# LayerNorm of a convolution branch inside a projection stage: gates loaded a chunk ahead, the next mean ahead of this variance, affine part on ScalarE

## The chip, the cores and the metric

The kernel runs on one core of a Trainium2 chip. The metric is device time in microseconds (us) for one execution. Engines: TensorE (PE, matmuls and transposes), VectorE (DVE), ScalarE (ACT), GpSimd (POOL) and SyncE (SP), whose queue issues the DMAs of this stage. Each engine takes its instructions in a fixed order that is set when the program is built.

## The reference, cut to what matters

One layer of a streaming encoder over a sequence of 2048 positions with 1024 channels. An input projection gives, among others, the input and the gate of a convolution branch (512 channels), queries, keys and values of an attention branch, its gate, and two merge gates. The branch that the change touches:

```
u = depthwise_causal_conv(glu(u), width 31) + b_dw
mu  = mean over 512 channels of u
xc  = u - mu
var = mean over channels of xc*xc
n   = xc * rsqrt(var + EPS) * ln_g + ln_b        # layer_norm
za  = silu(n) * silu(gate_A)                     # silu(n) = n * sigmoid(n)
y_A = za @ w_conv_out
```

Then stick-breaking attention over eight heads, the merge y = sigmoid(m_A) * y_A + sigmoid(m_B) * y_B, and the output projection with a residual.

## The kernel before, in words

All matmuls of the projections are in a split form: every float32 operand is a high part and a remainder, and a product is three matmuls (`mm3`, L135). Channels lie on the 128 partitions, the sequence is cut into four chunks of 512 columns (`CH`), and a projection block is one 128-channel slice of the output for one chunk: 24 matmuls of 512 columns into a PSUM tile `pd`, of which there are five.

The stages: inputs and modulation; projections with the convolution taps on VectorE (here the convolution's gates `ga` are computed, and stored to DRAM already as silu); then the stage of this case (L720 to L868); then attention, with the remaining merge gates as filler; then the output projections.

In the stage of this case three things are written by hand in turn. `v_group(5)` (L831) computes six half-blocks of values and stores them through tiles `st` (two of them, 128 x 1024); `gate_b(2)` and `gate_b(3)` compute the attention gate (L841), `merge_gate` three merge gate slices (L852). Each of these blocks ends in an evacuation by ScalarE (`vsg`, L847 or L858) and a store, and then calls `next(ln)`, which advances the generator `ln_all` (L775) by one step. So the LayerNorm of the four chunks is woven between blocks. Its steps for a chunk:

- mean: `ln_load` fetches four 128 x 512 tiles `cv` (one for each 128 channels, two sets); `presum` (L744) adds the four into `t1`, two on GpSimd (L747), two and the total on VectorE (L748, L749); `mean_in` splits the sum into `hl` (L770 on ScalarE, L771 on VectorE); two matmuls with a constant matrix of 1/512 give the mean on all partitions, `mub` (L783).
- centering: VectorE subtracts (L788), ScalarE squares (L790, into tiles `sq0` to `sq3`), `presum` adds the squares.
- three steps (blocks) later the variance: four narrow matmuls into `pst` (L798), EPS added (L800), an inverse square root by integer start and three Newton steps on 128 x 4 values (`rsqrt`, L81 to L93), four scaled identity matrices `dg` (L755).
- one block later (two for the second chunk) `spread` (L759) multiplies them with ones into `psb`: the inverse deviation on all partitions.
- normalizing, for each of the four tiles: VectorE multiplies by `psb` (L809); GpSimd applies gain and bias (L810); the convolution's gate is loaded into `gt`, a single tile (L814); ScalarE takes the Sigmoid into `lsg`, which has the buffer of that tile's square (L816); GpSimd multiplies (L817); VectorE multiplies by the gate (L819); SyncE stores `za` (L823).
- the mean of the next chunk (L825), and one more block.

The builder orders each engine's instructions from this program; within the stage TensorE is kept in the order that is written, and the other engines' work is fitted in by priority and by when operands come free. A tile that is allocated again waits for all uses of its former content.

Of the kernel before, what the change touches and what calls it, by code (L numbers as in the profile page):

```python
# [8 lines left out]
F32 = mybir.dt.float32  # L9
# [3 lines left out]
AF = mybir.ActivationFunctionType  # L13
ALU = mybir.AluOpType
# [4 lines left out]
P = 128  # L19
SEQ = 2048  # L20
D = 1024
KC = D // P
CH = 512
NCH = SEQ // CH
# [26 lines left out]
def trunk_kernel(  # L51
# [20 lines left out]
    nc = tc.nc  # L72
# [85 lines left out]
    ga_d = [[dram(f"ga{j}_{g}", [P, CH], F32) for g in range(NCH)] for j in range(JC)]  # L158
# [27 lines left out]
    with ExitStack() as s1:  # L186
# [221 lines left out]
        with tc.tile_pool(name="hx", reuse_waits="tile", bufs=1) as hx:  # L408
# [53 lines left out]
            for i in range(2):  # L462
# [5 lines left out]
                for k in (2 * i, 2 * i + 1):  # L468
# [4 lines left out]
                    else:  # L473
                        dve.scalar_tensor_tensor(out=sq, in0=xs[k], scalar=1.0, in1=xs[k],
                                                 op0=ALU.mult, op1=ALU.mult,
                                                 accum_out=ss[:, k:k + 1])
                if i == 0:
# [4 lines left out]
                                     op0=ALU.add, op1=ALU.mult)  # L482
# [14 lines left out]
            for kc in range(KC):  # L497
                col = slice(kc, kc + 1)
                if kc == 0:
                    cast(wq[0], w2_q0[0])  # L500
                act.activation(out=b_s[:, col], in_=mod[:, col], func=AF.Identity,
                               bias=ba[:, col])
# [217 lines left out]
        with ExitStack() as sl:  # L720
# [21 lines left out]
                return cv  # L742

            def presum(tiles):  # L744
                t1 = lp.tile([P, CH], F32, tag="t1", name="t1")
                t2 = lp.tile([P, CH], F32, tag="t2", name="t2")
                nc.gpsimd.tensor_tensor(out=t1, in0=tiles[0], in1=tiles[1], op=ALU.add)  # L747
                nc.vector.tensor_tensor(out=t2, in0=tiles[2], in1=tiles[3], op=ALU.add)  # L748
                nc.vector.tensor_tensor(out=t1, in0=t1, in1=t2, op=ALU.add)  # L749
                return t1  # L750
# [16 lines left out]
            def mean_in(cv):  # L767
                t1 = presum(cv)
                hl = lp.tile([P, 2, CH], F32R, tag="hl", name="hl")
                nc.scalar.copy(out=hl[:, 0, :], in_=t1)  # L770
                nc.vector.tensor_tensor(out=hl[:, 1, :], in0=t1, in1=f(hl[:, 0, :]),  # L771
                                        op=ALU.subtract)
                return hl

            def ln_all():  # L775
                cv = ln_load(ORDER[0])
                yield
                hl = mean_in(cv)
                yield
                for n_, g in enumerate(ORDER):  # L780
                    mub = pm.tile([P, CH], F32, tag="psb", name="mub")
                    for i in range(2):
                        mm(mub, onesr, hl[:, i, :], start=(i == 0), stop=(i == 1))  # L783
                    if n_ + 1 < NCH:
                        nxt = ln_load(ORDER[n_ + 1])
                    sqs = []
                    for j in range(JC):
                        nc.vector.tensor_tensor(out=cv[j], in0=cv[j], in1=mub, op=ALU.subtract)  # L788
                        sq = lp.tile([P, CH], F32, tag=f"sq{j}", name=f"sq{j}")
                        nc.scalar.activation(out=sq, in_=cv[j], func=AF.Square)  # L790
                        sqs.append(sq)
                    t1 = presum(sqs)
                    yield
                    yield
                    yield
                    vs = pm.tile([P, 4], F32, tag="pst", name="pst")
                    for i in range(4):
                        mm(vs[:, i:i + 1], t1[:, i * P:(i + 1) * P], invc, start=True, stop=True)  # L798
                    va = sm.tile([P, 4], F32, tag="va", name="va")
                    nc.vector.tensor_scalar(out=va, in0=vs, scalar1=EPS, scalar2=None,  # L800
                                            op0=ALU.add)
                    dg = diag(rsqrt(sm, va, 4, "lr"))
                    yield
                    if n_ == 1:
                        yield
                    rb = spread(dg)
                    for j in range(JC):
                        n = cv[j]
                        nc.vector.tensor_tensor(out=n, in0=n, in1=rb, op=ALU.mult)  # L809
                        nc.gpsimd.tensor_scalar(out=n, in0=n, scalar1=lng[:, j:j + 1],  # L810
                                                scalar2=lnb[:, j:j + 1], op0=ALU.mult,
                                                op1=ALU.add)
                        gt = lp.tile([P, CH], F32, tag="gt", name="gt")
                        nc.sync.dma_start(gt, ga_d[j][g])  # L814
                        sg = lp.tile([P, CH], F32, tag=f"sq{j}", name="lsg")
                        nc.scalar.activation(out=sg, in_=n, func=AF.Sigmoid)  # L816
                        nc.gpsimd.tensor_tensor(out=n, in0=n, in1=sg, op=ALU.mult)  # L817

                        nc.vector.tensor_tensor(  # L819
                            out=sg.rearrange("p (m t) -> p m t", t=2),  # L820
                            in0=gt.rearrange("p (m t) -> p m t", t=2),
                            in1=n.rearrange("p (t m) -> p m t", t=2), op=ALU.mult)
                        nc.sync.dma_start(za_d[j][g], sg)  # L823
                    if n_ + 1 < NCH:
                        hl = mean_in(nxt)  # L825
                        cv = nxt
                    yield

# [43 lines left out]
    with ExitStack() as s2:  # L872
# [35 lines left out]
        st = {}  # L908
# [323 lines left out]
```

## Time and profile before

| what | us |
|---|---|
| median of three runs (lowest, highest) | 1874.32 (1873.73, 1876.04) |
| the profiled execution's own time | 1877.81 |
| its span in the trace | 1876.1 |
| TensorE busy, share of the span | 1797.0, 96% |
| VectorE busy | 1228.2, 65% |
| ScalarE busy | 812.8, 43% |
| GpSimd busy | 681.3, 36% |
| TensorE busy from 640 to 800 us of the span | 149.36 of 160 |
| in the same stretch: VectorE, ScalarE, GpSimd | 72.71, 41.85, 61.42 |
| mean granted TensorE clock of the whole span | 0.993 |

The profile is one execution as the hardware profiler saw it. In its rows L817 is line 817 of the kernel, `a<-b` an instruction that writes tile a and reads tile b (the name `t` stands for `t1` and `t2`), and what stands in brackets or behind `<-` is idle time and who ended it. Matmul rows overlap. "Granted clock" is the share of full speed that TensorE was given. An engine's idle time costs nothing where another engine is the bound.

### The profile page before, as it was taken

Reading aid. Unit: us, or ns where it says so; the run is one execution under the profiler, and the core shown is the slowest. Engines: PE = TensorE matmul, PEld = TensorE weight load, DVE = VectorE, ACT = ScalarE, POOL = GpSimd, SP = SyncE. Lnnn points to the kernel's source line nnn. Section 1 sums busy time; section 2 is a strip of 40 time slices with the busy share of each in tenths; the row PEclk is TensorE's granted clock in tenths of the full one; section 3 lists DMA queues with packets and bytes.
Section 4 is the critical chain, followed back from the end, with each engine's and each line's share of the span. In section 5 each row is a group of like instructions: output and inputs, shape, how many; then the busy total and the mean of one; then the engine's idle time right before and its main releaser. Section 6 shows DMA issues by size and latency. Waiting matters only on the chain.

```text
span 1876.1 us, 27226 instructions
## 1 busy us (share of the span) xinstructions
PE 1797.0 (96%) x9612; PEld 1517.0 (81%) x9612; DVE 1228.2 (65%) x1696; ACT 812.8 (43%) x1880; POOL 681.3 (36%) x899
## 2 busy tenths in 40 slices
PE   6899999999999998999999999999999899999999
PEld 5888889899888977778877778777788677888887
DVE  7646578888879354467777777777777895334341
ACT  5465113232231122267766777776777752010110
POOL 0343111111121143466666666666666641010100
PEclk9999999999999999999999999999999999999999
DMA  8553402325132443432232323132322446353532
GB/s 288 169 186 105 137 29 80 90 67 148 45 104 93 157 141 118 149 128 81 79 96 68 102 63 109 61 93 70 99 65 88 131 143 215 107 163 96 164 95 79
DMA packets 117596, 211.08 MB, mean 113 GB/s; under 512 B 15442, under 2 KB 27730, under 8 KB 117460
## 3 DMA queue, kind: packets, MB, share of 16 engines
q1 hardware_dynamic: 116308, 207.24, 35.5%
q10 hardware_dynamic: 1152, 2.10, 0.3%
q8 instruction: 76, 1.25, 0.3%
q14 instruction: 60, 0.49, 0.1%
HBM read 137.98 MB, written 71.30 MB: 112 GB/s over the span
## 4 chain that ended last, share of the span: by engine, by line
PE 72%; DVE 8%; POOL 6%; issue 5%; DMA 5%; ACT 4%; SPq 1%; DVEq 0%; ACTq 0%; POOLq 0%
PE pd L115 38%; PE po L115 9%; PE p L115 8%; PE av L115 5%; PE pT L120 5%; PE z L115 5%; POOL w L952 3%; DVE sc L945 2%; POOL wlo L103 1%; ACT z L941 1%; DMA xt<-in_x_n_dram 1%; PE pt L120 1%; DVE tlo L979 1%; DMA wa<-in_w_ada_dram 1%; DMA gt<-ga 1%
## 5 line engine op out<-in xcount | busy, mean ns | idle before, releaser
L952 POOL TENSOR_TENSOR w<-w,sc 128x512 f32<-128x512 f32 (+1 forms) x320 | 361.6, 1130 | 251.8 <-DVE sc L945 179.1
L115 PE MATMUL pd<-hhi,whi 128*128 128x512 f32 x1024 | 413.4, 404 | 1.0 <-ACT vsg L858 1.0
L115 PE MATMUL pd<-hhi,wlo 128*128 128x512 f32 x1024 | 402.7, 393 | 0.0
L115 PE MATMUL pd<-hlo,whi 128*128 128x512 f32 x1024 | 402.5, 393 | 0.0
L945 DVE TENSOR_TENSOR_SCAN sc<-z,sc,w 128x512 f32<-128x512 f32 x192 | 245.0, 1280 | 90.9 <-ACT z L941 83.6
L103 POOL TENSOR_TENSOR wlo<-wl,whi 128x512 fp32r<-128x512 f32 x88 | 131.3, 1503 | 401.4 <-ACT whi L102 401.2
L115 PEld LDWEIGHTS pd<-hhi,wlo 128*128 128x128 f32 x1024 | 193.5, 189 | 42.5 <-POOL wlo L103 0.2
L940 ACT ACTIVATE w<-z 128x512 f32<-128x512 f32 (+1 forms) x320 | 172.2, 538 | 125.7 <-PE z L115 100.0
L115 PEld LDWEIGHTS pd<-hhi,whi 128*128 128x128 f32 x1024 | 195.5, 191 | 35.4 <-ACT vsg L858 1.4
L115 PEld LDWEIGHTS pd<-hlo,whi 128*128 128x128 f32 x1024 | 194.3, 190 | 34.3
L979 DVE TENSOR_TENSOR tlo<-pT,thi 128x512 fp32r<-128x512 f32 (+1 forms) x320 | 184.2, 598 | 35.8 <-ACT thi L978 32.4
L115 PE MATMUL z<-kt,q 128*128 128x512 f32 (+2 forms) x640 | 192.7, 382 | 5.0 <-DVE sc L945 3.5
L978 ACT CAST thi<-pT 128x512 fp32r<-128x512 f32 (+1 forms) x320 | 165.4, 527 | 61.3 <-PE pT L120 57.4
L120 PE MATMUL pT<-ident,w 128*128 128x128 f32 x1088 | 173.1, 275 | 9.8 <-POOL w L952 9.5
L120 PEld LDWEIGHTS pT<-ident,w 128*128 128x128 f32 x1088 | 137.5, 141 | 45.9 <-POOL w L952 14.5
L115 PE MATMUL pd<-whi,hhi 128*128 128x256 f32 x608 | 169.7, 287 | 3.6 <-ACT hhi L131 1.9
L941 ACT ACTIVATE z<-z 128x512 f32<-128x512 f32 (+1 forms) x320 | 171.7, 537 | 0.0
L115 PE MATMUL pd<-whi,hlo 128*128 128x256 f32 x608 | 167.0, 285 | 2.3 <-DVE hlo L131 1.7
L115 PE MATMUL pd<-wlo,hhi 128*128 128x256 f32 x608 | 154.0, 284 | 0.0
L949 DVE TENSOR_TENSOR_SCAN sc<-z,tri 128x512 f32<-128x512 f32 (+3 forms) x128 | 104.4, 819 | 53.9 <-ACT z L941 41.9
L115 PE MATMUL av<-tlo,vt 128*128 128x512 f32 (+1 forms) x320 | 123.2, 385 | 14.0 <-DVE tlo L979 10.9
L115 PEld LDWEIGHTS z<-kt,q 128*128 128x128 f32 x640 | 109.6, 189 | 24.1 <-DVE sc L945 5.4
(284 smaller groups left out, 3108.4 us busy)
## 6 DMA issues: line engine op xcount, KB each, us to landing
wl<-in_w_in_dram SPq DMA_DIRECT2D x64, 256.0 KB, 2.9
wa<-in_w_ada_dram SPq DMA_DIRECT2D x24, 512.0 KB, 5.1
wl<-in_w_qkv_dram SPq DMA_DIRECT2D x36, 256.0 KB, 2.7
xt<-in_x_n_dram SPq DMA_DIRECT2D x16, 512.0 KB, 5.5
vst<-st SPq DMA_DIRECT2D x64, 128.0 KB, 2.0
kt<-kst SPq DMA_DIRECT2D x32, 256.0 KB, 2.8
vt<-vst SPq DMA_DIRECT2D x32, 256.0 KB, 2.7
q<-qst SPq DMA_DIRECT2D x32, 256.0 KB, 2.8
```

The source lines that it names most:

```text
L103: (lo_eng or nc.gpsimd).tensor_tensor(out=lo[:, s], in0=wl, in1=f(hi[:, s]), op=ALU.subtract)
L115: i = nc.tensor.matmul(*a, **k)
L120: i = nc.tensor.transpose(*a)
L940: nc.scalar.activation(out=w[:, lo:], in_=z[:, lo:], func=AF.Sigmoid, scale=HD ** -0.5)
L941: nc.scalar.activation(out=z[:, lo:], in_=z[:, lo:], func=AF.Sigmoid, scale=-HD ** -0.5)
L945: nc.vector.tensor_tensor_scan(out=s[:, 1:], data0=z, data1=w, initial=s[:, 0:1], op0=ALU.mult, op1=ALU.bypass)
L949: nc.vector.tensor_tensor_scan(out=s[:, lo + 1:], data0=z[:, lo:], data1=tri[:, :CH - lo], initial=1.0, op0=ALU.mult, op1=ALU.max)
L952: nc.gpsimd.tensor_tensor(out=w[:, lo:], in0=w[:, lo:], in1=s[:, lo:CH], op=ALU.mult)
L978: nc.scalar.copy(out=thi[:, :n], in_=pT[:, :n])
L979: nc.vector.tensor_tensor(out=tlo[:, :n], in0=pT[:, :n], in1=f(thi[:, :n]), op=ALU.subtract)
```

## The change

Four edits. The gates of a chunk are loaded by a function of their own, two tiles of 128 x 1024 that take the places of the `st` tiles of the v stores (same pool, same tag), before the variance matmuls; the loads inside the normalizing loop are gone, and with them the tile `gt`. The next chunk's mean (`mean_in(nxt)`) stands behind the sum of this chunk's squares, instead of behind the normalizing; `t1` has two buffers for that. The affine on GpSimd is gone: the Sigmoid takes gain and bias as its per-partition scale and bias, and a second ScalarE instruction, Identity with the same scale and bias, writes the affine value. GpSimd's product and VectorE's gate product stay.

```diff
             def presum(tiles):
-                t1 = lp.tile([P, CH], F32, tag="t1", name="t1")
+                t1 = lp.tile([P, CH], F32, tag="t1", name="t1", bufs=2)
...
+            def gates(g):
+
+                gt = []
+                for i in range(2):
+                    t = vp.tile([P, D], F32, tag="st", name="gt", bufs=2)
+                    for j in range(2):
+                        gt.append(t[:, j * CH:(j + 1) * CH])
+                        nc.sync.dma_start(gt[-1], ga_d[2 * i + j][g])
+                return gt
...
                     t1 = presum(sqs)
+                    if n_ + 1 < NCH:
+                        hl = mean_in(nxt)
                     yield
                     yield
                     yield
+                    gt = gates(g)
                     vs = pm.tile([P, 4], F32, tag="pst", name="pst")
...
                         nc.vector.tensor_tensor(out=n, in0=n, in1=rb, op=ALU.mult)
-                        nc.gpsimd.tensor_scalar(out=n, in0=n, scalar1=lng[:, j:j + 1],
-                                                scalar2=lnb[:, j:j + 1], op0=ALU.mult,
-                                                op1=ALU.add)
-                        gt = lp.tile([P, CH], F32, tag="gt", name="gt")
-                        nc.sync.dma_start(gt, ga_d[j][g])
                         sg = lp.tile([P, CH], F32, tag=f"sq{j}", name="lsg")
-                        nc.scalar.activation(out=sg, in_=n, func=AF.Sigmoid)
+                        nc.scalar.activation(out=sg, in_=n, func=AF.Sigmoid,
+                                             scale=lng[:, j:j + 1], bias=lnb[:, j:j + 1])
+                        nc.scalar.activation(out=n, in_=n, func=AF.Identity,
+                                             scale=lng[:, j:j + 1], bias=lnb[:, j:j + 1])
                         nc.gpsimd.tensor_tensor(out=n, in0=n, in1=sg, op=ALU.mult)
...
-                            in0=gt.rearrange("p (m t) -> p m t", t=2),
+                            in0=gt[j].rearrange("p (m t) -> p m t", t=2),
...
                     if n_ + 1 < NCH:
-                        hl = mean_in(nxt)
                         cv = nxt
```

TensorE's rows are the same in both programs, in the same order. VectorE before, from the next mean's first addition to the middle of the first chunk's inverse square root (`st` are the v stores, `va` the variance, `lry` and `lrt` the Newton steps):

```order
L748 TENSOR_TENSOR t_6821<-cv_6527,cv_6529 128x512
L330 TENSOR_TENSOR st<-pd,st 128x8x64 x2
L800 TENSOR_SCALAR va<-pst 128x4
L85 TENSOR_SCALAR lry<-va 128x4
L89 SCALAR_TENSOR_TENSOR lrt<-lry 128x4
L330 TENSOR_TENSOR st<-pd,st 128x8x64
L91 TENSOR_TENSOR lrt<-lrt,va 128x4
L749 TENSOR_TENSOR t_6820<-t_6820,t_6821 128x512
```

and the same place on VectorE in the changed program:

```order
L748 TENSOR_TENSOR t_6549<-cv_6527,cv_6529 128x512
L749 TENSOR_TENSOR t_6548<-t_6548,t_6549 128x512
L330 TENSOR_TENSOR st<-pd,st 128x8x64
L771 TENSOR_TENSOR hl<-t_6548,hl 128x512
L330 TENSOR_TENSOR st<-pd,st 128x8x64
L813 TENSOR_SCALAR va<-pst 128x4
L85 TENSOR_SCALAR lry<-va 128x4
L89 SCALAR_TENSOR_TENSOR lrt<-lry 128x4
```

The first addition stood ahead of the variance already; the total (L749) and the remainder (L771) moved from the middle of the Newton steps to ahead of them.

SyncE's queue before, from the first chunk's first `za` store on (`ga_3_*` are the gates of the first chunk treated, `ga_2_*` of the second; `cv` are the inputs of the chunk after next):

```order
L823 DMA za_3_266<-lsg 128x512
L814 DMA gt<-ga_3_174 128x512
L740 DMA cv_6860<-cv_163 128x2x256
L849 DMA gb_2_193<-vsg 128x512
L823 DMA za_3_270<-lsg 128x512
L814 DMA gt<-ga_3_178 128x512
L740 DMA cv_6862<-cv_164 128x2x256
L823 DMA za_3_274<-lsg 128x512
L814 DMA gt<-ga_3_182 128x512
```

and SyncE's queue in the changed program, from the third and fourth gate of that chunk on:

```order
L782 DMA gt<-ga_3_178 128x512
L782 DMA gt<-ga_3_182 128x512
L859 DMA gb_3_194<-vsg 128x512
L101 DMA wl<-in_w_in_dram 128x512
L834 DMA za_3_266<-lsg 128x512
L834 DMA za_3_270<-lsg 128x512
L740 DMA cv_6858<-cv_163 128x2x256
L740 DMA cv_6860<-cv_164 128x2x256
L782 DMA gt<-ga_2_169 128x512
L834 DMA za_3_274<-lsg 128x512
L834 DMA za_3_278<-lsg 128x512
L859 DMA gb_2_193<-vsg 128x512
```

Stores and gate loads no longer alternate: all four gates of the chunk are queued ahead of its first store, and the first gate of the next chunk stands between this chunk's stores.

ScalarE before, in the first chunk's normalizing:

```order
L847 ACTIVATE vsg<-pd 128x512
L816 ACTIVATE lsg<-cv_6392 128x512
L816 ACTIVATE lsg<-cv_6394 128x512
L816 ACTIVATE lsg<-cv_6396 128x512
L816 ACTIVATE lsg<-cv_6398 128x512
L847 ACTIVATE vsg<-pd 128x512
```

and ScalarE at the same place in the changed program:

```order
L857 ACTIVATE vsg<-pd 128x512
L102 CAST whi<-wl 128x512
L824 ACTIVATE lsg<-cv_6392,lnb,lng 128x512
L824 ACTIVATE lsg<-cv_6394,lnb,lng 128x512
L826 ACTIVATE cv_6392<-cv_6392,lnb,lng 128x512
L826 ACTIVATE cv_6394<-cv_6394,lnb,lng 128x512
L824 ACTIVATE lsg<-cv_6396,lnb,lng 128x512
L824 ACTIVATE lsg<-cv_6398,lnb,lng 128x512
L826 ACTIVATE cv_6396<-cv_6396,lnb,lng 128x512
L826 ACTIVATE cv_6398<-cv_6398,lnb,lng 128x512
L857 ACTIVATE vsg<-pd 128x512
```

Four instructions became eight, Sigmoids and affines in pairs, between the evacuations of two projection blocks; the cast of a half of the next weights now stands ahead of them.

## The prediction

> **What bounds the kernel now.** I read the times first: three runs at 1873.73 to 1876.04 us, median 1874.32, and one profiled execution at 1877.81 us with a span of 1876.1. TensorE is busy 96% of it, so only time in which TensorE stands still, or runs slowly, can be won. TensorE executes the same instructions in the same order in both programs; the change can act only through what TensorE waits for. So the next view is the waits of TensorE, from 640 us to 800 us, the stretch in which the LayerNorm runs between projection blocks: engine, tile waited at, who released it, us in total, times, longest.
>
> ```profile
> PE pst L115 <- DVE t L749: 7.3, 3, 5.0
> PE psb L115 <- DVE dg L755: 2.4, 1, 2.4
> PE pd L115 <- ACT vsg L858: 1.0, 1, 1.0
> ```
>
> These are all its waits there: 10.7 us of 160. `pst` is the variance matmul, waiting for the sum of the squares; `psb` spreads the inverse deviation; the last wait stands at the hand-over to the attention stage and has nothing to do with the change. The timeline of TensorE gives the waits for `pst` singly (start, duration, idle time before in brackets); the third is what is left, 7.3 - 2.0 - 5.0, about 0.2 us.
>
> ```profile
> 693.60 1.05 PE L115 MATMUL pst<-invc,t 128*128 128x1 f32 x8 [2.04 <-DVE t L749]
> ...
> 735.51 1.86 PE L115 MATMUL pst<-invc,t 128*128 128x1 f32 x8 [5.03 <-DVE t L749]
> ```
>
> Then I cut out windows around the four waits. Columns: window, length, TensorE's busy time (instructions), granted clock, DMA share, GB/s.
>
> ```profile
> 664.00:674.00 10.00, 7.62 (x31) 0.83 0.36 116
> 690.00:700.00 10.00, 7.96 (x32) 0.83 0.35 127
> 730.00:746.00 16.00, 10.97 (x44) 0.79 0.26 90
> 766.00:776.00 10.00, 9.79 (x52) 1.00 0.39 130
> ```
>
> The clock falls after the three waits of 2 us and more, and not after that of 0.2. The loss is (1 - clock) x length: 1.7, 1.7 and 3.4 us, 6.8 in all. So the LayerNorm costs 9.7 us of idle TensorE and 6.8 us of slow TensorE: **16.5 us**, and no more can be won here.
>
> Why the sum of squares is late is read from the chain of waits around the longest case (start, us, what):
>
> ```profile
> 721.41 3.98 DMA gt<-ga
> 725.50 1.48 DVE lsg L819
> 727.41 2.81 DMA gt<-ga
> 730.34 0.72 DVE lsg L819
> 731.08 2.15 DMA za<-lsg
> 733.31 0.64 ACT sq L790
> 733.97 0.70 DVE t L748
> 734.77 0.70 DVE t L749
> 735.51 1.86 PE pst L115 x8
> 737.38 7.95 PE pd L115 x24
> ...
> 769.78 5.59 PE pd L115 x24
> ```
>
> There is one gate tile: a load, the product that frees it, the next load. The product's result `lsg` shares a buffer with the next chunk's square, so that square waits for the `za` store as well. The last two rows confirm the clock loss: the same 24 matmuls take 7.95 us behind the 5-us wait and 5.59 behind the 0.2-us one.
>
> **The change part by part.** How much time the chain has is TensorE's own work from one `psb` to the next `pst`: a block of 24 matmuls, `mub`, three more blocks.
>
> ```profile
> 707.13 1.05 PE L115 MATMUL psb<-dg,ones 128*128 128x128 f32 x8
> ...
> 713.51 0.63 PE L115 MATMUL mub<-hl,onesr 128*128 128x512 f32 x2
> ```
>
> From the end of `psb` at 708.18 to TensorE's arrival at `pst` at 735.51 - 5.03 = 730.48 are 22.3 us. The old chain needed 735.47 - 708.18 = 27.3. For the new one I need single durations: two groups (busy, mean ns of one), then the tile `lsg` (ns min/median/max, and us from issue to landing of its store).
>
> ```profile
> L809 DVE TENSOR_TENSOR cv<-cv,psb 128x512 f32<-128x512 f32 x16 | 9.9, 682 | 6.5 <-PE psb L115 6.5
> ...
> L399 ACT ACTIVATE hhi<-pt,b_s,a_s 128x512 fp32r<-128x512 f32 x24 | 17.6, 785 | 3.6 <-PE pt L120 3.5
> ```
>
> ```profile
> L817 POOL TENSOR_TENSOR cv<-cv,lsg x16: 1287/1296/1777, 670.3 to 784.5; 128x512 f32<-128x512 f32 x16
> L819 DVE TENSOR_TENSOR lsg<-gt,cv x16: 702/742/1527, 671.6 to 792.6; 128x512 f32<-128x512 f32 x16
> ...
> DMA to landing us min/median/max: 2.0/2.0/3.4
> ```
>
> *Gates ahead and affine part on ScalarE.* The new chain from `psb`: first product with the spread value 0.68; on ScalarE two Sigmoids and the first affine, 3 x 0.785 (both with per-partition scale and bias, a form the trace shows on L399; the affine's source there is PSUM, here SBUF, so this is the nearest row and not the thing itself) = 2.4; four GpSimd products in a row, 4 x 1.30 = 5.2, behind which the later affines keep up (8 x 0.785 = 6.3 against 2.4 + 3.9); the last gate product 0.74; store 0.3 + 2.0; square 0.64; two sums 1.4. Together 13.4 us against 22.3. With the longest durations of the rows (4 x 1.78, 1.53, 3.4) it is 17.5. All three waits for `pst` go, with 4.8 us to spare in the worse case. GpSimd loses sixteen affines, ScalarE gains sixteen instructions of about 0.8 us and 0.15 on each Sigmoid, some 15 us in 150; at the fewest it stands in front of evacuations of `pd`, of which five buffers hide 5.6 us each. Below nothing these edits can't go, since the loads and additions are the same bytes and sums.
>
> Where the gates could be late is the first chunk, because their tiles are the v stores' tiles: gates 2 and 3 wait on the sync queue until the last v stores have landed, and half of the weights of the projection after next queues behind them.
>
> ```profile
> 661.58 1.79 SPq L334 DMA_DIRECT2D vst<-st  x4
> ```
>
> Stores out at 663.4, landed 2.0 later, gate loads of 2.8 to 4.0 us: there at 669.4 at the latest. Their first use is after `psb` (arrival 664.15, end 665.2) + 0.7 + 2.4 + 3 x 1.3 = 672.2. Hidden by 2.8 us. The weights held up are used seven blocks of 5.5 us later. For later chunks the tiles' former content is a chunk old: no wait.
>
> *Next mean ahead of this variance.* Its last sum and its remainder leave the rsqrt chain on VectorE:
>
> ```profile
> 663.00 0.68 DVE L771 TENSOR_TENSOR hl<-t,hl 128x512 fp32r<-128x512 f32 x1
> 663.60 1.24 DVE L91 TENSOR_TENSOR lrt<-lrt,va 128x4 f32<-128x4 f32 x1
> 664.87 1.19 DVE L92 SCALAR_TENSOR_TENSOR lry<-lrt,lry 128x4 f32<-128x4 f32 x1
> 666.10 0.87 DVE L755 TENSOR_SCALAR dg<-ident,lry 128x128 f32<-128x128 f32 x4
> ```
>
> ```profile
> 663.47 2.56 POOL L103 TENSOR_TENSOR wlo<-wl,whi 128x512 fp32r<-128x512 f32 x2 [2.54 <-ACT whi L102]
> ```
>
> Two instructions of 0.68 leave, 1.4 us. The two 4-column steps of 1.2 us lie exactly under two GpSimd weight remainders; the remainders follow casts on ScalarE that stood behind this mean's cast and now don't, and the second of them waits for a later load, so at most one still meets the chain: another 1.2 us or more. 1.4 + 1.2 = 2.6 against the wait of 2.4: it goes, or leaves up to 1.2 us if both collisions stay. I take 0, since the spread starts on the first diagonal block and not on the fourth. A remnant that short cost no clock (the 0.2 and 1.0 waits). What is new behind VectorE's additions: they wait for the second pair of next chunk's inputs, and the variance is now queued behind that; see the last rival.
>
> **The sum** for the profiled execution: -7.3 - 2.4 - 6.8 = -16.5, 1877.81 to 1861.3. It lies 3.5 us above the median of the runs. I take that difference as the same for both kernels: 1874.32 - 16.5 = **1857.8 us**.
>
> A rule that would make it less: the Trainium skill, "TensorE: Matmul & The Clock Gate", section "HAM oscillation — how this bites in real kernels", says in essence that the array keeps full clock unless it idles for more than about 3.4 us. By it only the 5-us wait costs clock, and the sum would be 9.7 + 3.4 = 13.1 us, 1861.2. The trace differs: waits of 2.0 and 2.4 us were followed by the half clock too.
>
> **The rivals.**
> *Fewer clock losses in the timed runs.* If the 3.5 us between profile and median are the two losses of 1.7 us, absent there, 13.1 us are to be won: 1861.2. For it: the size fits. Against: the three runs lie within 2.3 us of each other, and losses that come and go would scatter them more. 14%.
> *A new wait on the chain.* GpSimd and VectorE block each other (663.60 and 663.47 above; an `lsg` of 1.53 us instead of 0.70). The four GpSimd products now run without a pause, beside the gate products. If each of these and of the four GpSimd products waits out the other, 4 x (1.3 + 1.5) = 11.2 us stand for 5.2 + 0.7, and 13.4 becomes 18.7: still under 22.3. Only with slow stores and ScalarE late too does TensorE wait, some 2 us and 1.7 of clock at each of three places, 11 us: 1868.9. 6%.
> The Trainium skill, "SBUF — State Buffer", section "SBUF: two separate sides", has this as an exclusive lock held for a whole instruction when a VectorE operation has two SBUF inputs and GpSimd reads SBUF too; the two collisions quoted agree.
> *Slower: the variance behind the next mean.* VectorE now adds the next chunk's inputs ahead of the variance. Their second pair is loaded behind a store of the block's own gate, about `psb` + 5.9 (block and `mub`) + 5 (VectorE's queue up to that store), and the sums stand some 3 us after landing. The slowest load of these inputs in the chain of waits:
>
> ```profile
> 625.01 5.67 DMA cv<-cv
> ```
>
> 10.9 + 5.7 + 3 = 19.6 of 22.3 us. Each us beyond idles TensorE, in the second and the third chunk. From a landing of some 8.4 us on it decides, from 13 on (4.9 us of idling and 3.4 of clock, twice) it costs more than the gain; at 17, 2 x (8.5 + 3.4) = 23.8 us go against 16.5: 1881.6. Against: it would take three times the slowest load, in a stretch that moves the same bytes as before. 2%.
> *The gates still come one by one.* If the scheduler put each load just ahead of its product, nothing would go: 1874.3. Against: the order of the sync queue has pairs of them a whole chunk ahead from the second chunk on. 3%.
>
> **How the numbers follow.** The likeliest case, all four waits and their clock losses gone, has 75%: 1857.8. Its own range is 1855.5 (lowest run instead of median, 0.6; the 1.0-us wait; 0.7 of scatter) to 1860 (a remnant of 1.2 us and 1 us of scatter). With the clock case it reaches to 1863.5, that is 1861.2 with the same remnant and scatter. Range 1855.5 to 1863.5; the last three cases are left out. A measurement here can tell 0.2%, 3.7 us, from no change. Faster: the first three cases less what of them is small, 0.93; within 0.2%: 0.04; slower: 0.03.
>
> **What would show it.** In the changed profile: no TensorE wait at `pst` or `psb` over 0.5 us in this stretch; a granted clock of 1.00 from 656 us to its end; the same 24-matmul block at 5.6 us everywhere; the squares no longer waiting for `za` stores for 3 us and more, gate products released by GpSimd and not by a load; affine steps of 0.7 to 0.8 us on ScalarE; the attention stage of the same length, begun 16 us earlier. A wait at `pst` from a sum released by GpSimd or ScalarE would show the second rival, a VectorE wait at the next mean's sum for a load the third; unchanged waits for gates the fourth. I am wrong if the stretch shortens by under 9 us, or if as much comes back in the attention stage.

## The result and the profile after

The changed kernel takes 1855.91 us in the median of five runs (1855.14 to 1858.59), beside 1874.32 us before (1871.32 to 1876.04, five runs): a ratio of 0.9907, 95% interval [0.9893, 0.9921]. A second set of five runs on another chip gave 1858.15 against 1874.19, 0.9912 [0.9896, 0.9928]. So the gain is 18.4 us once and 16.0 the other time, on both sides of the 16.5 that were forecast. The first median lies 1.9 us under the forecast 1857.8 and 0.4 above the lower end of the range.

These are the waits of TensorE from 624 to 790 us of the changed kernel's profiled execution (1858.59 us, span 1856.5), the stretch of the LayerNorm; the columns are us in total, times, longest:

```profile
PE pd L115 <- ACT vsg L868: 1.0, 1, 1.0
PE z L115 <- DVE sc L959: 0.8, 1, 0.8
```

No wait for `pst`, none for `psb`. The first of the two was there before as well; the second belongs to the attention stage, which begins earlier now and so falls into the window. Windows of the same execution show the clock (it is the number ahead of the DMA share): one over the whole stretch, and one around each of the two `pst` that had waited 2.0 and 5.0 us.

```profile
640.00:784.00 144.00, 143.02 (x728) 121.75 (x727) 76.72 (x141) 54.42 (x87) 49.01 (x37) 1.00 0.46 155
...
684.00:700.00 16.00, 16.00 (x80) 13.50 (x79) 7.20 (x22) 3.92 (x7) 2.52 (x2) 1.00 0.34 104
716.00:732.00 16.00, 16.00 (x80) 13.49 (x79) 8.61 (x24) 5.32 (x10) 0.00 (x0) 1.00 0.48 167
```

TensorE is busy 143.0 of 144 us at full clock. The chain of waits, which before ran through gate loads and products here, is now TensorE's own work without a gap (start, us, what):

```profile
656.93 0.79 PE pst L115 x8
657.71 5.55 PE pd L115 x24
663.27 0.97 PE psb L115 x8
664.24 5.50 PE pd L115 x24
669.73 0.47 PE mub L115 x2
670.20 16.34 PE pd L115 x72
686.54 0.79 PE pst L115 x8
```

I measure the stage from the start of the first `pst` to the first matmul of the attention filler, which is the row with the 0.98-us wait for `vsg` in both kernels. In TensorE's timeline, changed kernel first, then the kernel before:

```profile
656.76 0.95 PE L115 MATMUL pst<-invc,t 128*128 128x1 f32 x8
...
775.75 0.50 PE L115 MATMUL pd<-hhi,whi 128*128 128x512 f32 x1 [0.98 <-ACT vsg L868]
```

```profile
657.65 0.95 PE L115 MATMUL pst<-invc,t 128*128 128x1 f32 x8
...
793.62 0.50 PE L115 MATMUL pd<-hhi,whi 128*128 128x512 f32 x1 [0.98 <-ACT vsg L858]
```

The stage takes 775.75 - 656.76 = 118.99 us; before it was 793.62 - 657.65 = 135.97. That is 17.0 us of the 19.6 by which the two spans differ. The rest is 0.9 us ahead of the stage and 1.7 behind it, where both kernels run the same instructions.

What is not as forecast is the chain behind this. The one that leads to the third chunk's sum, from the end of the `psb` ahead of it at 699.25, on VectorE, ScalarE and GpSimd (rows of one kind that follow each other are one row; idle time and its releaser in brackets):

```profile
699.63 2.47 DVE L822 TENSOR_TENSOR cv<-cv,psb 128x512 f32<-128x512 f32 x4
704.04 3.53 DVE L830 TENSOR_TENSOR lsg<-gt,cv 128x512 f32<-128x512 f32 x2 [1.94 <-POOL cv L828]
707.49 1.27 DVE L798 TENSOR_TENSOR cv<-cv,mub 128x512 f32<-128x512 f32 x2
708.68 1.33 DVE L830 TENSOR_TENSOR lsg<-gt,cv 128x512 f32<-128x512 f32 x2
...
716.69 0.69 DVE L748 TENSOR_TENSOR t<-sq,sq 128x512 f32<-128x512 f32 x1 [4.88 <-ACT sq L800]
717.48 0.69 DVE L749 TENSOR_TENSOR t<-t,t 128x512 f32<-128x512 f32 x1
```

```profile
700.40 1.52 ACT L824 ACTIVATE lsg<-cv,lnb,lng 128x512 f32<-128x512 f32 x2 [1.41 <-DVE cv L822]
701.84 1.50 ACT L826 ACTIVATE cv<-cv,lnb,lng 128x512 f32<-128x512 f32 x2
...
710.00 0.63 ACT L800 ACTIVATE sq<-cv 128x512 f32<-128x512 f32 x1 [0.60 <-DMA za<-lsg]
715.02 0.63 ACT L800 ACTIVATE sq<-cv 128x512 f32<-128x512 f32 x1 [3.88 <-DMA za<-lsg]
715.55 0.58 ACT L868 ACTIVATE vsg<-pd 128x512 f32<-128x512 f32 x1
716.03 0.62 ACT L800 ACTIVATE sq<-cv 128x512 f32<-128x512 f32 x1
```

```profile
702.71 2.54 POOL L828 TENSOR_TENSOR cv<-cv,lsg 128x512 f32<-128x512 f32 x2 [14.47 <-ACT cv L826]
705.53 3.20 POOL L828 TENSOR_TENSOR cv<-cv,lsg 128x512 f32<-128x512 f32 x2 [0.28 <-ACT cv L826]
```

The sum is complete at 717.48 + 0.69 = 718.17, 18.9 us after `psb`; TensorE comes for it at 721.39, after 22.1. For the chunks before and after, the same subtraction gives 18.65 and 16.7. The first two gate products took 3.53 us together beside GpSimd's products; the last two, behind them and behind two subtractions of the next chunk (L798), 1.33. The squares still wait up to 3.9 us for a `za` store. Over all sixteen (ns min/median/max, then the store from issue to landing):

```profile
L824 ACT ACTIVATE lsg<-cv,lnb,lng x16: 801/803/819, 665.7 to 762.8; 128x512 f32<-128x512 f32 x16
L828 POOL TENSOR_TENSOR cv<-cv,lsg x16: 1290/1372/1783, 668.0 to 765.8; 128x512 f32<-128x512 f32 x16
L830 DVE TENSOR_TENSOR lsg<-gt,cv x16: 697/1790/1811, 669.3 to 768.1; 128x512 f32<-128x512 f32 x16
...
DMA to landing us min/median/max: 2.0/2.4/4.8
```

### The profile page after: what moved, and what is told of

The parts are those of the page before. It is cut to its first block, busy times and chain, and to the rows that moved or that the text cites. A ratio compares the mean times of both kernels' runs of the same rounds, so it can differ in the third digit from the quotient of the medians.

```text
span 1856.5 us, 27230 instructions
## 1 busy us (share of the span) xinstructions
PE 1788.4 (96%) x9612; PEld 1510.5 (81%) x9612; DVE 1229.2 (66%) x1696; ACT 825.9 (44%) x1896; POOL 668.6 (36%) x883
## 4 chain that ended last, share of the span: by engine, by line
PE 77%; DVE 7%; POOL 5%; ACT 4%; issue 4%; DMA 3%; SPq 0%; DVEq 0%; ACTq 0%; POOLq 0%
PE pd L115 43%; PE po L115 9%; PE p L115 8%; PE av L115 5%; PE pT L120 5%; PE z L115 5%; POOL w L962 3%; DVE sc L955 3%; DMA wl<-in_w_qkv_dram 1%; DVE tlo L989 1%; ACT z L951 1%; POOL wlo L103 1%; PE pt L120 1%; ACT w L950 1%; DMA qst<-qhi 1%
## 5 line engine op out<-in xcount | busy, mean ns | idle before, releaser
L115 PE MATMUL av<-tlo,vt 128*128 128x512 f32 (+1 forms) x320 | 122.8, 384 | 13.4 <-DVE tlo L989 10.2
```

What stands on the lines that cost most here:

```text
L115: i = nc.tensor.matmul(*a, **k)
```

## The experiments

The theory to be tested: the gates ahead take away the three `pst` waits and their clock losses, the mean ahead takes away the `psb` wait, and the affine part on ScalarE shortens the chain but isn't needed for it. Its rivals: the affine does the work (the single gate tile is late only because GpSimd is), or every edit brings a share wherever it stands. Six kernels hold one edit or two of the three; two lengthen the chain on purpose; four more settle what these left.

All in one table; "stage" is the length defined above, of the profiled execution of each; the waits are TensorE's at `pst` and `psb` in it. Before had medians of 1874.01 to 1874.19 beside them (17 to 27 runs each). One of the twelve first runs of affine only took 3575.78 us; the ratio is worked out without it, and the median of the other eleven is 1878.66.

| kernel | median, us (lowest to highest) | ratio to before [95%] | stage, us | `pst` waits | `psb` wait |
|---|---|---|---|---|---|
| before | 1874.32 (1871.32 to 1876.04) | 1 | 135.97 | 2.04, 5.03, 0.2 | 2.38 |
| changed kernel | 1855.91 (1855.14 to 1858.59) | 0.9907 [0.9893, 0.9921] | 118.99 | none | none |
| gates only | 1860.86 (1858.17 to 1863.11) | 0.9932 [0.9918, 0.9947] | 120.49 | none | 1.34 |
| mean only | 1871.47 (1869.09 to 1874.69) | 0.9985 [0.9976, 0.9995] | 130.63 | 2.20, 5.10 | none |
| affine only | 1879.1 (1873.97 to 1884.2, one 3575.78) | 1.0022 [1.0010, 1.0034] | 131.67 | 1.02, 3.88, 1.27 | 2.37 |
| gates and mean | 1858.6 (1857.71 to 1861.97) | 0.9920 [0.9907, 0.9933] | 118.99 | none | none |
| gates and affine | 1860.07 (1858.72 to 1861.58) | 0.9929 [0.9916, 0.9941] | 120.47 | none | 1.35 |
| mean and affine | 1874.02 (1872.9 to 1877.96) | 1.0006 [0.9997, 1.0014] | 133.21 | 2.64, 3.49, 1.23 | none |
| six additions | 1871.1 (1867.7 to 1872.98) | 0.9985 [0.9976, 0.9994] | 131.14 | 4.72, 2.86 | none |
| eight additions | 1874.01 (1870.27 to 1876.15) | 0.9997 [0.9988, 1.0006] | 135.76 | 5.80, 3.65, 0.27 | none |
| changed kernel again | 1858.15 (1856.15 to 1858.93) | 0.9912 [0.9896, 0.9928] | 118.91 | none | none |
| gates and mean again | 1858.42 (1858.02 to 1860.6) | 0.9918 [0.9903, 0.9933] | 118.97 | none | none |
| product on VectorE | 1856.45 (1855.32 to 1857.58) | 0.9905 [0.9887, 0.9923] | 118.89 | none | none |
| affine only again | 1878.31 (1874.41 to 1882.01) | 1.0024 [1.0012, 1.0036] | 135.11 | 1.84, 4.15, 1.2 | 2.37 |

### Gates ahead alone

From the changed kernel, mean and affine put back:

```diff
-                    if n_ + 1 < NCH:
-                        hl = mean_in(nxt)
                     yield
...
+                        nc.gpsimd.tensor_scalar(out=n, in0=n, scalar1=lng[:, j:j + 1],
+                                                scalar2=lnb[:, j:j + 1], op0=ALU.mult,
+                                                op1=ALU.add)
-                        nc.scalar.activation(out=sg, in_=n, func=AF.Sigmoid,
-                                             scale=lng[:, j:j + 1], bias=lnb[:, j:j + 1])
-                        nc.scalar.activation(out=n, in_=n, func=AF.Identity,
-                                             scale=lng[:, j:j + 1], bias=lnb[:, j:j + 1])
+                        nc.scalar.activation(out=sg, in_=n, func=AF.Sigmoid)
...
                     if n_ + 1 < NCH:
+                        hl = mean_in(nxt)
```

> Gates loaded ahead alone; the mean and the affine on GpSimd as before. Theory (the single gate tile with its load, product, load made the squares late; the mean inside the rsqrt made the spread late): the three waits for pst go, 7.3 us, with the clock lost behind two of them, 5.1 us; the wait for psb in the first chunk stays with 2.4 us and 1.7 us of clock. 12 to 13 us faster than before, about 1862. Rival (the affines on GpSimd make the chain long): at least the two long waits for pst stay in part, under 7 us faster, 1868 or more.

13.2 us of gain in the median (1874.01 to 1860.86), with no `pst` wait left. TensorE's waits in the stage:

```profile
PE psb L115 <- DVE dg L755: 1.3, 1, 1.3
PE pd L115 <- ACT vsg L867: 1.0, 1, 1.0
```

The `psb` wait is 1.34 us, not before's 2.38, and the clock stayed at 1.00 behind it. I had expected it whole. In before's inverse square root two steps on four columns (L91, L92) took 1.2 us each beside two GpSimd weight remainders in a row. Here the second remainder comes at 664.60, 3.5 us after the first, and only one step is slow:

```profile
661.19 1.23 DVE L91 TENSOR_TENSOR lrt<-lrt,va 128x4 f32<-128x4 f32 x1
662.46 0.16 DVE L92 SCALAR_TENSOR_TENSOR lry<-lrt,lry 128x4 f32<-128x4 f32 x1
```

So this one edit carries most of the gain: three waits of 7.3 us and the losses behind them, and the loss behind `psb` too.

### Next mean ahead alone

From the kernel before. Its sum lies in the tile `dg`, which is free at that time, since a second `t1` has no room beside `gt`:

```diff
-                t1 = presum(cv)
+                dg = lp.tile([P, 4, P], F32, tag="dg", name="dg", bufs=1)
+                t1 = presum(cv, dg.rearrange("p a b -> p (a b)"))
...
                     t1 = presum(sqs)
+                    if n_ + 1 < NCH:
+                        hl = mean_in(nxt)
...
-                        hl = mean_in(nxt)
                         cv = nxt
```

> The next mean ahead of the variance alone; gates one by one and the affine on GpSimd as before. The mean's sum is kept in the tile of the scaled identities, since a second buffer for t1 has no room while the gate tile is there. Theory: the wait for psb (2.4 us) and its clock loss (1.7) go, the waits for pst stay within 1 us each: 4 us faster, about 1870. Rival (two GpSimd weight remainders, not the mean, hold the rsqrt up): over 1 us of the wait for psb stays and the time moves by under 2 us, 1872 to 1875.

2.5 us in the median (1874.01 to 1871.47) where 4 were expected, and 5.3 us of the stage (135.97 to 130.63). The `psb` wait is gone, the two long `pst` waits stand as they were, and the clock halves behind them as before:

```profile
687.19 1.05 PE L115 MATMUL pst<-invc,t 128*128 128x1 f32 x8 [2.20 <-DVE t L750]
...
729.15 1.86 PE L115 MATMUL pst<-invc,t 128*128 128x1 f32 x8 [5.10 <-DVE t L750]
```

The sum of squares is not freed by this edit: it still stands behind the gates.

### Affine part on ScalarE alone, twice

From the kernel before:

```diff
-                        nc.gpsimd.tensor_scalar(out=n, in0=n, scalar1=lng[:, j:j + 1],
-                                                scalar2=lnb[:, j:j + 1], op0=ALU.mult,
-                                                op1=ALU.add)
...
-                        nc.scalar.activation(out=sg, in_=n, func=AF.Sigmoid)
+                        nc.scalar.activation(out=sg, in_=n, func=AF.Sigmoid,
+                                             scale=lng[:, j:j + 1], bias=lnb[:, j:j + 1])
+                        nc.scalar.activation(out=n, in_=n, func=AF.Identity,
+                                             scale=lng[:, j:j + 1], bias=lnb[:, j:j + 1])
```

> The affine on ScalarE alone; gates one by one, mean as before. Theory: the waits for pst stay as they are, since the gate loads in turn set them; each first product comes about 1 us later or earlier, which the next loads pass on: 1872 to 1876, no change that can be told. Rival (GpSimd's work sets the chain): four affines of 0.8 us leave the chain of each chunk, the waits of 2.0 and 5.0 us become 0 and about 2, and the clock losses shrink with them: 6 to 8 us faster, about 1867.

> The affine part on ScalarE alone, once more, for a second profiled execution. Its median lay 5 us above the one before, while its profiled execution, at 1873.97 the fastest of all, showed a stage shorter by 4 us. If the loss lies in the stage (gates that come later and miss more often), this execution, if it is an ordinary one of 1878 to 1880, shows pst waits of over 8 us in all or a second z wait for q; if it lies elsewhere, the stage is again about 132 us long and the time is lost outside of it. Median 1876 to 1880.

Slower both times, by 0.22% and 0.24%, 4 to 5 us, where no change was expected the first time. In the chain of waits of the second execution, the single gate tile is what bounds it, as before, with one thing worse (start, us, what):

```profile
711.21 1.81 DVE lsg L819
...
713.45 2.88 DMA gt<-ga
...
716.42 1.86 DVE lsg L819
```

```profile
L819 DVE TENSOR_TENSOR lsg<-gt,cv x16: 700/1360/1852, 670.6 to 792.6; 128x512 f32<-128x512 f32 x16
```

The products `lsg` that give the gate tile free take 1.36 us in the median, 0.74 before. The first of these two runs beside GpSimd's second product (its first two take from 709.89 to 712.43 without a pause, since no affine stands between them), the second beside a weight remainder of GpSimd that starts at 716.41. A product of 1.8 us delays the next load by 1.1 us. A new wait stands behind the stage, for loads of the attention stage. The last `za` store, which is ahead of them in SyncE's queue, goes out 2.7 us after the stage's end here and 0.3 us before it in the kernel before:

```profile
PE z L115 <- DMA q<-qst: 2.3, 2, 2.0
```

That fits with an edit that wins nothing. It doesn't account for the 4 to 5 us: the two profiled executions (1873.97 and 1876.04 us) are among the fastest of theirs, and their stages, 131.67 and 135.11, are not longer than before's. Where the ordinary ones of 1878 to 1880 lose their time stays open.

### Two edits of three

"Gates and mean" leaves the affine on GpSimd (the affine part of the first diff above), "gates and affine" leaves the mean late (its other part), "mean and affine" joins the last two diffs.

> The whole change but for the affine, which stays on GpSimd. Theory (the affine's move is worth nothing by itself): no wait for pst or psb over 0.5 us, the time of the changed kernel within 1.5 us, 1855 to 1858. Rival (with the affines on GpSimd the eight operations in a row, 4 x 0.8 and 4 x 1.3 us, with the collisions on VectorE use up the 3 us that the changed kernel has to spare): a wait for pst of 1 to 3 us in the second and third chunk, with clock losses, 1859 to 1865.

> The whole change but for the mean, which stays behind the normalizing. Theory: only the wait for psb in the first chunk is left, 2.4 us with 1.7 of clock: 4 us slower than the changed kernel, about 1860. Rival (the mean's place also sets the later chunks): further waits at mub or pst, 1863 or more.

> Mean ahead and affine on ScalarE, gates one by one into the single tile (mean's sum kept in the tile of the scaled identities). Theory: the waits for pst of before stay, no wait for psb: 1869 to 1874. Rival (the affine's move shortens the chain once the mean is out of the way): under 4 us of waits for pst, 1866 or less.

Gates and mean have the stage of the changed kernel to the hundredth, 118.99 us, without the affine. Gates and affine have that of the gates alone (120.47 and 120.49). Mean and affine without the gates are no faster than before, and 2.5 us slower than the mean alone: the `pst` waits are 7.4 us in all, as with the mean alone (7.3), but each of the two longest is followed by 6.8 us of half clock, where with the mean alone the first is followed by 3.4; and the wait for `q` stands behind the stage again.

```profile
PE pst L115 <- DVE t L750: 7.4, 3, 3.5
PE z L115 <- DMA q<-qst: 2.0, 2, 1.6
```

So the rival that each edit brings a share wherever it stands has fallen, and the one that the affine does the work too. The medians of the changed kernel and of gates and mean, 1855.91 and 1858.6, left 2.7 us open. Both ran once more, unchanged, on one chip:

> The changed kernel once more, unedited, so that it stands beside gates-and-mean on the same chip. If the affine part on ScalarE is worth nothing on top of the two other edits (my theory: TensorE waits for nothing in the stage in either), the two medians agree within 1.5 us and the stage from the first pst to the attention filler is 119.0 us in both. If the 2.7 us between their medians so far (1855.9 and 1858.6, other chips) are real, this one is faster by 2 to 3 us again.

> Gates ahead and mean ahead with the affine part left on GpSimd, once more. My theory: the same as the changed kernel within 1.5 us. Rival (GpSimd's sixteen affines of 1.3 us cost something outside the stage's TensorE waits): slower by 2 to 3 us.

1858.15 and 1858.42 us, stages of 118.91 and 118.97: beside the two others the affine part is worth 0.3 us, far less than the scatter of the runs. Without it the gate products take less, 0.74 us in the median: beside one, GpSimd is often in an affine, and there it is the affine that takes longer (1.33 us instead of 0.77). GpSimd's own chain is longer for it; the sums of the second and third chunk come 19.7 and 17.9 us after `psb`, 18.6 and 19.3 in the changed kernel of this pair: one later, one earlier.

### The chain lengthened

If TensorE waits for nothing because the sum comes in time, a later sum must bring the waits back. Additions without effect (the larger of a number and itself) behind the sum, from the changed kernel, six or eight:

```diff
                         hl = mean_in(nxt)
+                    for _ in range(6):
+                        nc.vector.tensor_tensor(out=t1, in0=t1, in1=t1, op=ALU.max)
                     yield
```

> The changed kernel with six additional VectorE instructions behind the sum of the squares (the maximum of that sum with itself, 0.7 us each), which the variance waits for. Chain and arrival in the changed kernel leave 3.5, 3.2 and 5.4 us in the second, third and fourth chunk. Theory: waits for pst of about 1.1 us in the second and third chunk, none in the fourth, and no clock lost behind waits this short: 2 to 2.5 us slower than the changed kernel. Rival (any wait of 1 us costs clock): 1.7 us more for each, 5 to 6 us slower.

> The same with eight such instructions. Theory (a wait of 2 us is enough for the half clock, as in the kernel before): waits for pst of about 2.5 us in the second and third chunk, 0.3 in the fourth, and 1.7 us of clock lost behind each of the two long ones: 8 to 9 us slower than the changed kernel. Rival (the clock falls only after an idle time of about 3.4 us): the same waits, granted clock of 1.00 behind them, 5 to 5.5 us slower.

The waits came back, and with eight the whole gain is gone (1874.01 us). But the sizes were wrong. With six I expected two waits of 1.1 us and there were 4.72 and 2.86; with eight two of 2.5, and there were 5.80 and 3.65. So whether waits of 1 us cost clock was not tested here; behind all four the clock halved. VectorE's rows ahead of the first of these waits:

```profile
683.67 1.60 DVE L749 TENSOR_TENSOR t<-t,t 128x512 f32<-128x512 f32 x1
685.30 0.69 DVE L806 TENSOR_TENSOR t<-t 128x512 f32<-128x512 f32 x1
685.91 0.68 DVE L748 TENSOR_TENSOR t<-cv,cv 128x512 f32<-128x512 f32 x1
...
689.64 1.75 DVE L806 TENSOR_TENSOR t<-t 128x512 f32<-128x512 f32 x1
691.32 0.68 DVE L860 TENSOR_TENSOR vsg<-pd,vsg 128x512 f32<-128x512 f32 x1
691.92 0.67 DVE L806 TENSOR_TENSOR t<-t 128x512 f32<-128x512 f32 x1
```

The sum itself (L749) was complete at 685.27, 19.6 us after `psb` and not 18.7, since it took 1.60 us beside a weight remainder of GpSimd. The six (L806) then took 7.3 us, to 692.59, and not six times 0.69: VectorE works in its fixed order, so the next mean's sums and remainder and an evacuation (`vsg`) stand between them, and one of the six took 1.75 beside the next remainder. What is put into a chain costs what is woven into it as well.

### The product on VectorE

To see what makes the gate products slow, from the changed kernel:

```diff
-                        nc.gpsimd.tensor_tensor(out=n, in0=n, in1=sg, op=ALU.mult)
+                        nc.vector.tensor_tensor(out=n, in0=n, in1=sg, op=ALU.mult)
```

> The changed kernel with the sixteen products n * sigmoid(n) on VectorE in place of GpSimd. If the gate products of 1.7 to 1.8 us are slow because GpSimd's product runs at the same moment and each waits for the other, they fall to 0.70 to 0.75 here, the new products take 0.70 each, and the chain from the end of psb to the last sum shortens from 16.7-18.9 us to some 14 to 15. If they are slow by themselves (a strided operand read from the new gate tiles), they stay at 1.7. The time in both cases is that of the changed kernel within 2 us, since TensorE has no wait at pst there to lose.

```profile
L828 DVE TENSOR_TENSOR cv<-cv,lsg x16: 679/685/694, 666.2 to 763.7; 128x512 f32<-128x512 f32 x16
L830 DVE TENSOR_TENSOR lsg<-gt,cv x16: 701/712/720, 667.0 to 764.4; 128x512 f32<-128x512 f32 x16
```

The same products of the same tiles take 0.712 us in the median, 0.720 at the most. So their 1.79 us were GpSimd's products at the same moment, not the gate tiles or the strided operand. The Trainium skill, "SBUF — State Buffer", section "SBUF: two separate sides", describes it: the loser of the shared port waits until the other's instruction has ended. The trace agrees (0.71 and 1.79). The chain became shorter by less than expected, 17.3 and 16.7 us instead of 14 to 15, since the squares still wait for the stores, which took up to 4.7 us to land. The time, 1856.45 us, is that of the changed kernel: there is no wait left to win.

## Why the prediction was right, and where its steps were not

- **The bound and the sum, 16.5 us.** Right. The stage became 17.0 us shorter; the waits of 9.7 us are gone and the clock losses of 6.8 with them, as the windows at 1.00 show: together the 16.5. The other 0.5 us of the stage, and the 2.6 us by which the two profiled spans differ outside it, were not part of the forecast.
- **"With 4.8 us to spare in the worse case."** Wrong in size: it was 3.5, 3.2 and 5.4 us, where 8.9 were the likely value. Three terms of the 13.4 us were too small. In the third chunk the last gate product ended 10.8 us after `psb`, where 9.0 were summed: GpSimd's first product began 3.5 us after `psb` and not 3.1, its four products took 6.0 us beside the gate products and not 5.2, and the last gate product, with the third in front of it, ended 1.3 us behind them and not 0.7. From there to the landed store that the third square waits for were 5.0 us instead of 2.3: the third and fourth stores went out at 710.25, behind three loads in SyncE's queue. In the last chunk, where no loads stand beside them, the stores landed in 2.0 to 2.4 us. Behind that came two squares with an evacuation between them, 1.6 us instead of 0.64. 10.8 + 5.0 + 1.6 + 1.5 = 18.9. The sum with the longest values of before's rows (17.5) was too small by the store (5.0 for 3.7) and the second square: the change itself brought loads, stores and products together. That the squares no longer wait 3 us for a `za` store was a sign that the prediction named, and it did not come: one waited 3.9.
- **Gates and affine as one term.** The text let both together take away the `pst` waits. The runs part them: the gates do it alone, the affine adds nothing.
- **The `psb` wait, 2.4 us and its 1.7 of clock.** It went, with no remnant, as taken. But it went with nothing to spare: `psb` began 0.15 us after the first diagonal block was ready, at 662.96, the same distance as before behind its wait. And the mean's share depends on the rest. Alone it takes 5.3 us off the stage. With the gates ahead only 1.5 are left for it (120.49 to 118.99), since these take away one of the two slow Newton steps, and the 1.34 us that remain of the wait cost no clock.
- **First chunk's gates.** Right: no gate product of the changed kernel waited for a load; the 8.3 us that VectorE stood idle ahead of them were all ended by GpSimd's products.
- **Fewer clock losses in the timed runs.** Did not come: 18.4 and 16.0 us were won, not 13.1. In the second set the granted clock of the runs is 0.993 in the mean before and 0.996 in the changed kernel; 0.003 of 1874 us are some 5 us, so the timed runs had such losses too. The 3.5 us between the profiled execution and the median are scatter and no constant: the changed kernel's two profiled executions lie 2.7 us above and 1.5 below the medians of their sets, with stages of 118.99 and 118.91.
- **A new wait on the chain.** Its mechanism, VectorE and GpSimd blocking each other, was there for ten of the sixteen gate products (1.2 to 1.8 us each); together with late stores it used up two thirds of the likely slack at the most. Its own sum, 18.7 us, is close to the 18.9 measured, but by luck: it held all four gate products slow and the stores on time.
- **The variance behind the next mean.** No wait came of it. Its price was put too early: the sum of the inputs delays `va` and not `pst`, so TensorE would wait only at `psb`, a block later. In both runs of gates and mean the sums of the next inputs ended 22.5 to 22.9 us after `psb`, past the 22.3 that I gave, and cost nothing.
- **The clock rule** of the Trainium skill ("TensorE: Matmul & The Clock Gate", section "HAM oscillation — how this bites in real kernels"), by which only idle time of over 3.4 us costs clock, would have made it 13.1 us. The waits of 1.84 to 2.86 us in these runs were followed by the half clock as well; the measured sum stands.

## What to carry to other kernels

Where one buffer makes a load wait for the last use of its former content, loading ahead into more buffers is worth more than faster steps: the gates ahead brought 15.5 of the 17.0 us of the stage, and taking work off the engine beside that chain (the affine) brought nothing, or, while the buffer was still single, a loss whose cause stayed open. The edit gives four places instead of one and issues the loads earlier; no run tells these two apart. A slack worked out from the single durations of the old profile is too large when the change itself brings two engines or several transfers to the same moment; the nearest row for such a step is one that already collides. And before a step is called a gain of its own, it should be tried without its neighbours: of three edits one carried the gain, one a tenth of it behind the first and 5.3 us of the stage alone, one none.

## What the runs showed of the hardware that was not expected

**The clock is lost in portions of 3.4 us at half speed, and not at once.** In the second execution with the affine alone TensorE waited from 690.03 to 691.87. In windows of 1 us behind that, the clock is the number ahead of the DMA share:

```profile
692.00:693.00 1.00, 1.00 (x9) 1.00 (x10) 0.58 (x2) 0.00 (x0) 0.00 (x0) 1.00 0.73 229
693.00:694.00 1.00, 1.00 (x5) 0.82 (x5) 1.00 (x3) 0.00 (x0) 0.99 (x1) 0.89 0.76 289
694.00:695.00 1.00, 1.00 (x4) 0.80 (x3) 0.99 (x3) 0.00 (x0) 0.29 (x1) 0.50 0.50 193
...
697.00:698.00 1.00, 1.00 (x5) 0.79 (x5) 0.96 (x5) 0.00 (x0) 0.00 (x0) 0.90 0.00 0
```

The half clock begins 1.9 us after the matmuls did (0.89 in that window: at 693.78) and ends at 697.2 (0.90), 3.4 us later: 1.7 us lost. From the first `pst` into the attention stage, over all profiled executions, no wait of 0.2 to 1.35 us cost any clock; of the two longer waits for `q` in the attention stage, that of 1.61 us (mean and affine) cost a portion and that of 1.99 (above) none; waits of 1.84 to 2.86 in the stage cost one portion, but for one of 2.64 that cost two; those from 3.49 to 5.10 one or two, and that of 5.80 three. Behind the longest the half clock can begin before the matmuls do (eight additions: at 689.35, with the wait until 691.96), and that part costs nothing.

So what decides is not the length alone, but how the wait lies. Two places outside the stage show it too. The same wait of 1.75 us for `sg`, some 35 us ahead of the stage, is in all fourteen profiled executions; the half clock followed in one (six additions, at 622.92) and not in the other thirteen. And in the changed kernel three waits of 0.61, 0.50 and 1.26 us, from 1458.7 to 1463.5, were followed by it at 1463.48: short waits that lie close together can cost clock. All portions of an execution start on one grid. In the kernel before those of the stage start at 667.25, 694.56 and 735.52, that is 27.31 = 8 x 3.413 and 40.96 = 12 x 3.413 us apart; the starts in every other execution that has more than one are whole multiples of 3.413 us apart as well.

The Trainium skill ("TensorE: Matmul & The Clock Gate", section "What's actually happening") speaks of free-running windows of 3.4 us. The portions and the grid agree. A window without any work was not needed: some 2 us of idle time were enough at most places, but not at the wait of 1.99, and why stays open.

**A 256-KB store took from 2.0 to 4.8 us to land** within one stage, with the same bytes. The median was 2.0 before and with gates and mean, 2.4 in the changed kernel and 3.2 with the product on VectorE. In the changed kernel the slow ones are the third and fourth stores of the first three chunks (3.6 to 4.8 where the landing is in the trace), which go out behind loads of inputs and gates; the fourth of the last chunk, without such loads, took 2.1.
